# Hybrid decoder block on one core: expert rows stored at once by GpSimd's queue, and gathered back with an add inside the DMA

## The chip, the cores and the metric

The kernel runs on one core of one Trainium2 chip. The metric is the device time of one execution in microseconds (us), as the median of several runs; lower is better. The profile shows one execution on that core: TensorE (PE, with its weight loads PEld), VectorE (DVE), ScalarE (ACT), GpSimd (POOL) and SyncE (SP), and the DMA queues. SP's DMAs run in queue q1, GpSimd's in queue q0.

## The reference, cut to what matters

A decoder block for 512 tokens of width 1024. A token mixer and a LayerNorm come first; the change lies in the mixture of experts (16 experts in 4 groups, two experts for each token) and the last LayerNorm.

```python
# t: (512, 1024) after the first LayerNorm; combine: the two gates of each token, 0 elsewhere
h = jax.nn.silu(einsum("td,edf->tef", t, expert_w_gate)) * einsum("td,edf->tef", t, expert_w_up)
h = h * combine[:, :, None]
y = einsum("tef,efd->td", h, expert_w_down)          # expert_w_*: 1024 x 256, 256 x 1024
out = layer_norm(ALPHA * t + y, ln2_g, ln2_b)
```

Only the two chosen experts of a token count, so the kernel computes each expert on the at most 128 rows that chose it (an overflow branch, not taken here, does the rest).

## The kernel before

**Stages.** Up to about 650 us the kernel does the mixer, the first LayerNorm and the router. HT (four tiles of 128 tokens x 1024, float32) holds the normalized rows, with the last residual in it; hD is its copy in HBM. Then comes a loop over the experts, `for e in range(NE)`, and after it the last LayerNorm, tile by tile.

**The expert loop.** All float32 matmuls are done as three passes on split operands (high part, low part). Iteration e does, in an order written out by hand (`K` keeps it): `gate_up(e + 1, 0)`, the transposes of expert e's activations (L1303) and their split by ACT (L1304) and DVE (L1305, the low part FHL), `turn(e + 2, 0)`, `gate_up(e + 1, 1)`, `turn(e + 2, 1)`, `swiglu(e + 1)`, and `down(e, 0)`, `down(e, 1)`, whose passes need FHL. Between them stand three `splits()`, each of which splits one 1 MiB piece of weights (ACT L805 makes the high part, DVE L809 the low part, two of each).

**Weights.** Three pieces of 1 MiB for each expert, 48 in all, go through a ring of 16 raw buffers (`GR_RAW`); SP issues the DMAs (`eload`). When PE has used piece n, `release()` frees its buffer and issues the next load. From e = 3 on, five of the releases are withheld (`owed`): the ring shrinks to 11 buffers, and the 10 slots of 4 KB each are `kept`, nine for the expert outputs yo[3] to yo[11] and one for OHR.

**Token rows.** `gather(e)` is an indirect DMA of GpSimd that brings expert e's 128 rows from hD into one of five slots, XG[e % 5]. The `turn`s of an expert read its slot.

**Outputs of experts 0 to 11.** ACT scales the output into yo[e] (L1237). Experts 0 to 2 write into the gather slot XG[(e + 2) % 5] and SP stores it to yD in HBM at once; experts 3 to 11 stay in SBUF, and nine stores follow SP's last weight load (L1171). At the end of iteration 13 GpSimd issues eight indirect gathers of yD rows (L1347), two for each tile of 128 tokens, into buffers YG. Five of the eight gathered tiles are added to HT by GpSimd (L1352), three by DVE (two at L1309, one at L1399).

**Outputs of experts 12 to 15** never leave SBUF. They are put back to their tokens by matmuls with one-hot matrices, OHT[m], in `rows_of_last` (L1254). DVE makes OHT[m] at L1334 at the end of iterations 10 to 13, from OHR, a broadcast of the ranks out of HBM (rkD) that SP loads in one DMA at e = 3.

**The end.** For each tile i: `total(i)` adds the PSUM sums to HT (DVE L1364 twice, L1365) and ACT takes the squares; `inv_std(i)` (DVE L1372 to L1376); `half2(i)` finishes columns up to W2[i] on DVE (L1384) and the rest on ACT (L1383) and GpSimd (L1385, L1386), and SP stores both; `half1(i + 1)` (DVE L1379) starts the next tile. W2 is 512, 576, 704, 832. The order on DVE is total 0, (L1399), half1 0, then for each i: total i+1, inv_std i, half2 i, half1 i+1.

Of the kernel before, what the change touches and what calls it, by code (L numbers as in the profile page):

```python
# [13 lines left out]
BF16 = mybir.dt.bfloat16  # L14
I32 = mybir.dt.int32
AF = mybir.ActivationFunctionType
ALU = mybir.AluOpType
AX = mybir.AxisListType

D = 1024  # L20
S = 512
NT = 4
H = 8
KT = 8
NE = 16
# [5 lines left out]
CAP = 128  # L31
# [5 lines left out]
def body(ctx: ExitStack, tc: tile.TileContext, P: dict, out):  # L37
    nc = tc.nc
    V, A, G, T, SP = nc.vector, nc.scalar, nc.gpsimd, nc.tensor, nc.sync
# [24 lines left out]
    def reg(kb, *shape, dt=F32):  # L64

        n = int(np.prod(shape))
        o = int(round(kb * 256))
        assert o + n <= n_all, (kb, shape)
        return shaped(place(o, n, dt), shape)
# [22 lines left out]
    def carve(off, shape, dt, parts=128):  # L92
        half = dt in (F16, BF16)
        n = int(np.prod(shape))
        w = (n + 1) // 2 if half else n
        assert off + w <= n_all, (off, shape)
        return shaped(place(off, n, dt, parts), shape), off + -(-w // 8) * 8
# [42 lines left out]
    K = tc.keep_in_program_order  # L140
# [161 lines left out]
    p = pb()  # L302
# [5 lines left out]
    p = pb()  # L308
# [10 lines left out]
    early = [coff[0]]  # L319
# [21 lines left out]
    p = pb()  # L341
# [16 lines left out]
    p = pb()  # L358
# [47 lines left out]
    for h in range(H):  # L406
        if h % 2 == 0:
            w = wload(wcol("k", h // 2)) if h else w_k0
        p = chan_tile(w, h % 2)
        silu = conv_silu(p, 8 + h, KTr[:, h])  # L410
        p = pkk[h] = pb()
# [42 lines left out]
    for t in range(31):  # L454

        n, m = 31 - t, t + 1
# [21 lines left out]
    for cch in range(4):  # L478
# [3 lines left out]
        for j in range(2):  # L482
            h = cch * 2 + j
            p = chan_tile(w, j)
            conv_silu(p, h, QTr[:, h])
            p = pb()
# [4 lines left out]
            p = pb()  # L491
# [43 lines left out]
    for cch in range(4):  # L535
# [3 lines left out]
        for j in range(2):  # L539
            h = cch * 2 + j  # L540
            p = chan_tile(w, j)
            vT = scratch(S)
            conv_silu(p, 16 + h, vT)
            p = pb()
# [20 lines left out]
    for c in range(NT):  # L565
        cs = slice(c * 128, (c + 1) * 128)
        if c < NT - 1:
            for hh in range(2):
                hs = slice(hh * 4, hh * 4 + 4)
                p = pb()  # L570
# [3 lines left out]
        for hh in range(2):  # L574
            hs = slice(hh * 4, hh * 4 + 4)
            if c > 0:
                p = pb()
                for u in range(4):
                    T.matmul(p[:, u * 128:(u + 1) * 128], KTr[:, hh * 4 + u, cs], SS[:, hh * 4 + u], start=True, stop=True)
                for u in range(4):  # L580
                    h = hh * 4 + u
                    V.scalar_tensor_tensor(VT[:, c, h], p[:, u * 128:(u + 1) * 128], nG[:, h, c:c + 1], VT[:, c, h],
                                           op0=ALU.mult, op1=ALU.add)
                p = pb()
# [5 lines left out]
            p = pb()  # L590
# [3 lines left out]
            if c < NT - 1:  # L594
                p = pb()
# [4 lines left out]
                else:  # L600
                    for u in range(4):
                        h = hh * 4 + u
                        V.scalar_tensor_tensor(SS[:, h], SS[:, h], GL[:, h, c:c + 1], p[:, u * 128:(u + 1) * 128],
                                               op0=ALU.mult, op1=ALU.add)
            p = pb()
# [9 lines left out]
    for cch in range(4):  # L615
        w = wload(wcol("u", cch))
        for j in range(2):
            p = chan_tile(w, j)
# [18 lines left out]
    for c in range(NT):  # L637
# [4 lines left out]
        for h in range(H):  # L642
            V.scalar_tensor_tensor(QK[:, c, h], QK[:, c, h], ory[:, c, h:h + 1], Z[:, c, h * 128:(h + 1) * 128],
                                   op0=ALU.mult, op1=ALU.mult)
        for hh in range(2):
            hs = slice(hh * 4, hh * 4 + 4)
            p = pb()
# [16 lines left out]
    for hh in range(2):  # L664
        p = pb()
# [4 lines left out]
    for hh in range(2):  # L670
        p = pb()
        T.matmul(p, ones, WST[:, hh * 4:hh * 4 + 4], start=True, stop=True)
        for u in range(4):
            gi = hh * 4 + u
            V.scalar_tensor_tensor(EG[:, gi], p[:, u * 128:(u + 1) * 128], colT[:, 104 + gi:105 + gi], EG[:, gi],
                                   op0=ALU.mult, op1=ALU.add)
# [40 lines left out]
    for gi in range(8):  # L717
        p = pb()
        with tc.issue_after(done[23].ins):
            for i in range(NT):  # L720
# [4 lines left out]
                               op0=ALU.mult, op1=ALU.add)  # L725
# [9 lines left out]
    HT = reg(120, NT, D)  # L735
    for i in range(NT):
        SP.dma_start(HT[:, i, :], x_in[:, i, :])
    for cch in range(4):
        cols = slice(cch * 256, (cch + 1) * 256)
        if cch:  # L740
            w1 = wload(wcol("gdn", cch))
            for j in range(2):
                p = chan_tile(w1, j)
                A.activation(SIG[j], p, AF.Sigmoid)
        w2 = wload(P["w_dn_out"][0][:, cols])
        for j in range(2):
            p = chan_tile(w2, j, lambda k: OHI[:, :, k], lambda k: OLO[:, :, k])
            V.tensor_tensor(YT[j], p, SIG[j], ALU.mult)
        w3 = wload(wcol("gsgu", cch))
        for j in range(2):  # L750
            p = chan_tile(w3, j)
            A.activation(SIG[j], p, AF.Sigmoid)
        w4 = wload(P["w_sgu_out"][0][:, cols])
        for j in range(2):
            n = cch * 2 + j
            p = chan_tile(w4, j, lambda k: GHI[:, k], lambda k: UG[k][1])
# [17 lines left out]
    free, at, nload, last_load = deque(GR_RAW), {}, [0], [None]  # L774

    def eload():

        n = nload[0]
        if n >= len(order):
            return  # L780
        nload[0] += 1
        e, part = order[n]
        kb = at[n] = free.popleft()
        if part < 2:
            raw, lo = both(kb, 4, 512)
            ks = slice(part * 512, part * 512 + 512)
            SP.dma_start(raw[:, :, 0:FF], P["expert_w_gate"][0][e][ks].rearrange("(k p) f -> p k f", p=128))
            SP.dma_start(raw[:, :, FF:512], P["expert_w_up"][0][e][ks].rearrange("(k p) f -> p k f", p=128))
        else:
            raw, lo = both(kb, 2, D)  # L790
            last_load[0] = SP.dma_start(raw, P["expert_w_down"][0][e].rearrange("(k p) d -> p k d", p=128))
        raws[order[n]] = raw, lo
# [44 lines left out]
    p = pb()  # L837
# [40 lines left out]
    iof, irb, pid = late(16), late(128, dt=BF16), late(1)  # L878
# [135 lines left out]
    NL = 12  # L1014
    sli, idx, gsl = cst(NT, 2, dt=I32), cst(16, dt=I32), cst(16)
# [13 lines left out]
    p = pb()  # L1029
# [8 lines left out]
    XG = [reg(o, D) for o in (184, 188, 192, 0, 4)]  # L1038

    def gather(e):  # L1040
        if e < NE:
            return G.indirect_dma_start(out=XG[e % 5], out_offset=None, in_=hD,  # L1042
                                        in_offset=bass.IndirectOffsetOnAxis(ap=idx[:, e:e + 1], axis=0))
# [32 lines left out]
    with tc.If(most > CAP):  # L1076
# [12 lines left out]
        with tc.For_i(0, NE, 1) as eo:  # L1089
            wex = lambda nm, r: P[nm][0][bass.ds(eo, 1)].rearrange("o (k p) f -> p (o k) f", p=128)[:, r]  # L1090
            for b in range(1, NBLK):
                SP.dma_start(oi, iD[bass.ds(eo * (NBLK - 1) + (b - 1), 1)].rearrange("b p o -> p (b o)"))
                G.indirect_dma_start(out=OX, out_offset=None, in_=hD,
                                     in_offset=bass.IndirectOffsetOnAxis(ap=oi[:, 0:1], axis=0))
                for hh in range(2):
                    p = pb()
# [4 lines left out]
                p = pa()  # L1101
# [9 lines left out]
                p = pb()  # L1111
# [5 lines left out]
                for n in range(2):  # L1117
                    p = pa()
# [46 lines left out]
    FHL = carve(mixer_only, (2, 128), F32R)[0]  # L1165
    yD = dram.tile([ZROW + 1, D], F32, name="yD")
    Y_LAST, yo = [], {}
    E0 = 3

    def store(e):  # L1170
        SP.dma_start(yD[e * CAP:(e + 1) * CAP], yo[e])  # L1171

    OHT = [regr(o, S) for o in (188, 190, 192, 194)]
    def turn(e, hh):
# [9 lines left out]
        K(V.tensor_tensor(XGL[:, hs], v3(p), f_(XGH[:, hs]), ALU.subtract))  # L1184

    pgu = {}
    used, owed, kept = [0], [0], deque()

    def release():

        n = used[0]
        used[0] += 1
        if n == 0:
            return
        if owed[0]:
            owed[0] -= 1
            kept.extend((at[n], at[n] + 4))
        else:
            free.append(at[n])
            eload()  # L1200

    def kmm3(*args):
        K(T.matmul(args[0], args[1], args[3], start=args[5], stop=False))  # L1203
# [14 lines left out]
    def down(e, n):  # L1218
        wh, wl = ready[(e, 2)]
        p = pa()  # L1220
        ns = slice(n * 512, (n + 1) * 512)
        for f in range(2):
            kmm3(p, FHH[:, f], FHL[:, f], wh[:, f, ns], wl[:, f, ns], f == 0, f == 1)
        if n == 1:
            release()
        w_ = gsl[:, e:e + 1]
        if e >= NL:
            if n == 0:
                kb = free.popleft()
                Y_LAST.append((regr(kb, D), regr(kb + 4, D)))  # L1230
            yh, yl = Y_LAST[e - NL]
            K(A.activation(yh[:, ns], p, AF.Copy, scale=w_))
            K(V.scalar_tensor_tensor(yl[:, ns], p, w_, f_(yh[:, ns]), op0=ALU.mult, op1=ALU.subtract))
            return
        if n == 0:
            yo[e] = reg(kept.popleft(), D) if e >= E0 else XG[(e + 2) % 5]
        K(A.activation(yo[e][:, ns], p, AF.Copy, scale=w_))  # L1237
        if n == 1 and e < E0:
            store(e)

    def swiglu(e):
# [48 lines left out]
    A.activation(rkT, p[:(NE - NL) * NT, :128], AF.Copy)  # L1290
    SP.dma_start(rkD, rkT)
    for e in range(NE):
        if E0 <= e < NL and (e == E0 or not (e - E0) % 2 == 0):
            owed[0] += 1
        gate_up(e + 1, 0)
        if e == NE - 2:
            LNR2 = reg(free.pop(), 2, D)
            ln_rows("ln2_g", "ln2_b", LNR2)
        if e < NE - 2:
            splits()  # L1300
        p = pb()
        for f in range(2):
            K(T.transpose(p[:, f * 128:(f + 1) * 128], SGB[:, f * 128:(f + 1) * 128], ident))  # L1303
        K(A.activation(FHH, v3(p[:, 0:256]), AF.Copy))  # L1304
        K(V.tensor_tensor(FHL, v3(p[:, 0:256]), f_(FHH), ALU.subtract))  # L1305
        turn(e + 2, 0)
        if e == NE - 1:
            for n in range(2):
                K(V.tensor_tensor(HT[:, 0], HT[:, 0], YG[0][n], ALU.add))  # L1309
            rows_of_last(1, 0, (0, 1))  # L1310
        gate_up(e + 1, 1)
        splits()
        turn(e + 2, 1)
        if e <= E0:
            gather(e + 5)
        if e == E0:
            gather(e + 6)
        if e >= E0:
            gather(e + 7)
        if e == E0:  # L1320
            kept_rk = kept.popleft()
            OHR = reg(kept_rk, NE - NL, NT, 128, dt=BF16)
            SP.dma_start(OHR, bass.AP(tensor=rkD.tensor, offset=rkD.offset,
                                      ap=[[0, 128], [NT * 128, NE - NL], [128, NT], [1, 128]]))
        swiglu(e + 1)
        splits()
        down(e, 0)
        down(e, 1)
        if e == NE - 2:
            rows_of_last(0, 0, (0, 1))  # L1330
            rows_of_last(0, 1, (0, 1))
        if NL - 2 <= e < NE - 2:
            m = e - NL + 2
            K(V.tensor_scalar(OHT[m], OHR[:, m].rearrange("p i t -> p (i t)"), pid, None, op0=ALU.is_equal))  # L1334
        if e == NL:
            with tc.issue_after(last_load[0].ins):
                for m in range(E0, NL):
                    store(m)
        if e == NE - 3:
            YG = [yo[m] for m in range(E0, NL)] + [reg(kept_rk, D)]  # L1340
            while len(YG) < 8:
                kb = free.popleft()
                YG += [reg(kb, D), reg(kb + 4, D)]
            YG = [YG[i * 2:i * 2 + 2] for i in range(NT)]
            for i in range(NT):
                for n in range(2):
                    K(G.indirect_dma_start(out=YG[i][n], out_offset=None, in_=yD,  # L1347
                                           in_offset=bass.IndirectOffsetOnAxis(ap=sli[:, i, n:n + 1], axis=0)))
            for i in range(1, NT):
                for n in range(2):  # L1350
                    if i + n > 1:
                        K(G.tensor_tensor(HT[:, i], HT[:, i], YG[i][n], ALU.add))  # L1352


    out_v = out.rearrange("b (i p) d -> p (b i) d", p=128)
# [40 lines left out]
        rows_of_last(i, n, ALL, pool)  # L1396
    W2 = [512, 576, 704, 832]
    total(0)
    K(V.tensor_tensor(HT[:, 1], HT[:, 1], YG[1][0], ALU.add))  # L1399
    half1(0, W2[0])  # L1400
    for i in range(NT):
        if i + 1 < NT:
# [27 lines left out]
```

## Time and profile before

| | |
|---|---|
| time, median of 3 runs (lowest, highest) | 830.06 us (829.65, 832.38) |
| time of the profiled execution | 829.64 us |
| its span, first to last instruction | 827.9 us |
| busy of the span: PE, DVE, ACT, POOL | 94%, 65%, 46%, 13% |
| moved by DMA | 133.65 MB, mean 161 GB/s |
| of that by q1 (SP) and q0 (GpSimd) | 120.33 MB and 12.58 MB |
| mean granted clock of TensorE | 0.976 of full speed |

The profiled execution's time is 1.74 us more than its span; a change of the span is taken as a change of the time. Shares over the whole span are means over stages with different limits, so the expert loop (about 650 to 800 us) and the end (800 to 827.9 us) have to be read each for itself.

### The profile page before, as it was taken

How to read it: one execution, taken by the hardware profiler on the slowest of the kernel's cores; microseconds unless marked ns; L12 is line 12 of the kernel's file. 1: busy time of each engine (PE TensorE's matmuls, PEld its weight loads, DVE VectorE, ACT ScalarE, POOL GpSimd, SP SyncE). 2: the span in 40 equal slices, each digit the busy share in tenths (PEclk: the TensorE clock that was granted, in tenths of full speed). 3: DMA queues.
4: the chain of work that ended last, by engine and by line, in shares of the span. 5: the costliest groups of instructions: out<-in, count | busy, mean ns of one | idle time of the engine just before them, and what ended most of it. 6: DMA issues, size and time to landing. Idle time of an engine off the chain costs nothing.

```text
span 827.9 us, 10853 instructions
## 1 busy us (share of the span) xinstructions
PE 779.1 (94%) x4043; PEld 647.5 (78%) x4043; DVE 535.5 (65%) x1026; ACT 385.0 (46%) x612; POOL 106.7 (13%) x90
## 2 busy tenths in 40 slices
PE   8879999999999999999999999999994999999991
PEld 7567888787889988888788888888773788888780
DVE  3337882997575992547633332323578899999987
ACT  2485353453335542423322222222323899899843
POOL 0002002001100000000500000001031202110177
PEclk9998999999999999999999999999996999999996
DMA  9526336336260135343244333369818899999762
GB/s 225 87 59 169 79 81 143 84 69 154 46 139 2 51 72 95 94 102 77 99 129 103 103 101 103 102 241 331 291 52 260 297 382 388 367 341 307 280 250 101
DMA packets 110752, 133.65 MB, mean 161 GB/s; under 512 B 19780, under 2 KB 93032, under 8 KB 110696
## 3 DMA queue, kind: packets, MB, share of 16 engines
q1 hardware_dynamic: 107240, 120.33, 50.2%
q0 software_dynamic: 3456, 12.58, 4.3%
q8 instruction: 33, 0.54, 0.3%
q14 instruction: 23, 0.19, 0.1%
HBM read 120.82 MB, written 12.08 MB: 161 GB/s over the span
## 4 chain that ended last, share of the span: by engine, by line
PE 76%; issue 9%; DVE 9%; DMA 2%; ACT 2%; POOL 1%; POOLq 0%; DVEq 0%; SPq 0%; ACTq 0%
PE pa L237 16%; PE pa L236 16%; PE pa L235 16%; PE pa L1205 5%; PE pa L1203 4%; PE pa L1204 4%; PE pb L1181 2%; PE pb L525 1%; DVE r L809 1%; DVE r L386 1%; PE pb L607 1%; PE pb L592 1%; PE pb L509 1%; DMA r<-hD,r 1%; PE pb L414 1%
## 5 line engine op out<-in xcount | busy, mean ns | idle before, releaser
L235 PE MATMUL pa<-r,r 128*128 128x512 f32 (+1 forms) x712 | 280.1, 393 | 7.5 <-ACT r L149 7.3
L236 PE MATMUL pa<-r,r 128*128 128x512 f32 (+1 forms) x712 | 278.3, 391 | 2.2 <-DVE r L150 2.2
L237 PE MATMUL pa<-r,r 128*128 128x512 f32 (+1 forms) x712 | 277.5, 390 | 0.0
L150 DVE TENSOR_TENSOR r<-r,r 128x2048 fp32r<-128x2048 f32 (+2 forms) x48 | 102.8, 2148 | 134.6 <-ACT r L149 134.6
L235 PEld LDWEIGHTS pa<-r,r 128*128 128x128 f32 x712 | 134.4, 189 | 35.6 <-ACT r L149 8.1
L236 PEld LDWEIGHTS pa<-r,r 128*128 128x128 f32 x712 | 134.5, 189 | 29.5 <-DVE r L150 3.2
L237 PEld LDWEIGHTS pa<-r,r 128*128 128x128 f32 x712 | 134.3, 189 | 27.3 <-DVE r L232 0.4
L149 ACT ACTIVATE r<-r 128x2048 fp32r<-128x2048 f32 (+2 forms) x48 | 84.8, 1777 | 143.3 <-PE pa L236 82.0
L809 DVE TENSOR_TENSOR r<-r,r 128x1024 fp32r<-128x1024 f32 x96 | 117.1, 1222 | 5.6 <-ACT r L805 3.9
L805 ACT ACTIVATE r<-r 128x1024 fp32r<-128x1024 f32 x96 | 96.3, 1059 | 0.0
L1203 PE MATMUL pa<-r,r 128*128 128x512 f32 x192 | 78.2, 407 | 0.0
L1205 PE MATMUL pa<-r,r 128*128 128x512 f32 x192 | 75.9, 395 | 1.0 <-DVE r L1305 1.0
L1204 PE MATMUL pa<-r,r 128*128 128x512 f32 x192 | 75.6, 394 | 0.0
L386 DVE SCALAR_TENSOR_TENSOR r<-pa,r,r 128x511 f32<-128x511 f32 (+2 forms) x72 | 53.5, 743 | 15.7 <-ACT r L384 15.2
L1205 PEld LDWEIGHTS pa<-r,r 128*128 128x128 f32 x192 | 36.0, 188 | 9.9 <-DVE r L1305 1.9
L1203 PEld LDWEIGHTS pa<-r,r 128*128 128x128 f32 x192 | 36.3, 189 | 7.1 <-ACT r L1183 0.2
L1204 PEld LDWEIGHTS pa<-r,r 128*128 128x128 f32 x192 | 36.3, 189 | 6.9
L387 ACT ACTIVATE r<-r 128x512 f32<-128x512 f32 x24 | 15.1, 630 | 46.7 <-DVE r L386 42.9
L1042 POOL DMA_INDIRECT r<-hD,r x16 | 21.1, 1317 | 91.4 <-PE pb L1181 37.3
L758 POOL TENSOR_TENSOR r<-r,r 128x512 f32<-128x512 f32 x8 | 10.3, 1290 | 146.2 <-DVE r L757 142.0
L384 ACT ACTIVATE r<-pa,r 128x512 f32<-128x512 f32 x24 | 16.3, 680 | 25.2 <-PE pa L237 25.2
L1181 PE MATMUL pb<-r,r 128*128 128x128 f32 x128 | 20.2, 284 | 8.3 <-DMA r<-hD,r 8.2
(325 smaller groups left out, 899.0 us busy)
## 6 DMA issues: line engine op xcount, KB each, us to landing
r<-in_w_in_dram SPq DMA_DIRECT2D x29, 1024.0 KB, 8.9
r<-in_expert_w_gate_dram SPq DMA_DIRECT2D x32, 512.0 KB, 6.8
r<-in_expert_w_down_dram SPq DMA_DIRECT2D x16, 1024.0 KB, 8.4
r<-in_expert_w_up_dram SPq DMA_DIRECT2D x32, 512.0 KB, 8.4
yD<-r SPq DMA_DIRECT2D x12, 512.0 KB, 9.7
r<-in_x_dram SPq DMA_DIRECT2D x8, 512.0 KB, 5.9
r<-in_w_dn_out_dram SPq DMA_DIRECT2D x4, 1024.0 KB, 5.5
r<-in_w_sgu_out_dram SPq DMA_DIRECT2D x4, 1024.0 KB, 6.0
```

Source lines behind the costliest of these rows:

```text
L149: pin(A.activation(hi, raw, AF.Copy))
L150: pin(eng.tensor_tensor(lo, raw, f_(hi), ALU.subtract))
L235: pin(T.matmul(o, lh, rh, start=first, stop=False))
L236: pin(T.matmul(o, lh, rl, start=False, stop=False))
L237: pin(T.matmul(o, ll, rh, start=False, stop=last))
L386: V.scalar_tensor_tensor(acc[:, s:], p[:, :S - s], wc(3 - s), acc[:, s:], op0=ALU.mult, op1=ALU.add)
L805: K(A.activation(hi[:, s], raw[:, s], AF.Copy))
L809: K(V.tensor_tensor(lo[:, s], raw[:, s], f_(hi[:, s]), ALU.subtract))
L1181: K(T.transpose(p[:, u * 128:(u + 1) * 128], XG[e % 5][:, k * 128:(k + 1) * 128], ident))
L1203: K(T.matmul(args[0], args[1], args[3], start=args[5], stop=False))
L1204: K(T.matmul(args[0], args[1], args[4], start=False, stop=False))
L1205: K(T.matmul(args[0], args[2], args[3], start=False, stop=args[6]))
```

## The change

Every expert from 0 to 11 now writes its output into the gather slot XG[(e + 2) % 5], and GpSimd's queue, no longer SP's, stores it at once. No weight buffer is withheld, so the ring keeps 16 buffers. `gather(e + 5)` is issued in iteration e throughout. Behind expert 11's store GpSimd issues the eight gathers from yD, now with an add in the DMA, straight onto HT: first one for each of the four tiles, then the second ones. All additions of gathered rows by DVE and GpSimd go. OHR becomes four DMAs of 128 KiB, issued by SP in iteration 11; three of the four lie in slot XG[2] (192 to 195 KB), which holds yo[10] until it is stored. The OHT[m] are made one iteration later, at the end of iterations 11 to 14.

```diff
--- before.py
+++ after.py
@@ -1165,10 +1165,9 @@
     FHL = carve(mixer_only, (2, 128), F32R)[0]
     yD = dram.tile([ZROW + 1, D], F32, name="yD")
     Y_LAST, yo = [], {}
-    E0 = 3
 
     def store(e):
-        SP.dma_start(yD[e * CAP:(e + 1) * CAP], yo[e])
+        K(G.dma_start(yD[e * CAP:(e + 1) * CAP], yo[e]))
 
     OHT = [regr(o, S) for o in (188, 190, 192, 194)]
     def turn(e, hh):
@@ -1184,7 +1183,7 @@
         K(V.tensor_tensor(XGL[:, hs], v3(p), f_(XGH[:, hs]), ALU.subtract))
 
     pgu = {}
-    used, owed, kept = [0], [0], deque()
+    used = [0]
 
     def release():
 
@@ -1192,12 +1191,8 @@
         used[0] += 1
         if n == 0:
             return
-        if owed[0]:
-            owed[0] -= 1
-            kept.extend((at[n], at[n] + 4))
-        else:
-            free.append(at[n])
-            eload()
+        free.append(at[n])
+        eload()
 
     def kmm3(*args):
         K(T.matmul(args[0], args[1], args[3], start=args[5], stop=False))
@@ -1233,9 +1228,9 @@
             K(V.scalar_tensor_tensor(yl[:, ns], p, w_, f_(yh[:, ns]), op0=ALU.mult, op1=ALU.subtract))
             return
         if n == 0:
-            yo[e] = reg(kept.popleft(), D) if e >= E0 else XG[(e + 2) % 5]
+            yo[e] = XG[(e + 2) % 5]
         K(A.activation(yo[e][:, ns], p, AF.Copy, scale=w_))
-        if n == 1 and e < E0:
+        if n == 1:
             store(e)
 
     def swiglu(e):
@@ -1290,8 +1285,6 @@
     A.activation(rkT, p[:(NE - NL) * NT, :128], AF.Copy)
     SP.dma_start(rkD, rkT)
     for e in range(NE):
-        if E0 <= e < NL and (e == E0 or not (e - E0) % 2 == 0):
-            owed[0] += 1
         gate_up(e + 1, 0)
         if e == NE - 2:
             LNR2 = reg(free.pop(), 2, D)
@@ -1305,23 +1298,18 @@
         K(V.tensor_tensor(FHL, v3(p[:, 0:256]), f_(FHH), ALU.subtract))
         turn(e + 2, 0)
         if e == NE - 1:
-            for n in range(2):
-                K(V.tensor_tensor(HT[:, 0], HT[:, 0], YG[0][n], ALU.add))
             rows_of_last(1, 0, (0, 1))
         gate_up(e + 1, 1)
         splits()
         turn(e + 2, 1)
-        if e <= E0:
-            gather(e + 5)
-        if e == E0:
-            gather(e + 6)
-        if e >= E0:
-            gather(e + 7)
-        if e == E0:
-            kept_rk = kept.popleft()
-            OHR = reg(kept_rk, NE - NL, NT, 128, dt=BF16)
-            SP.dma_start(OHR, bass.AP(tensor=rkD.tensor, offset=rkD.offset,
-                                      ap=[[0, 128], [NT * 128, NE - NL], [128, NT], [1, 128]]))
+        gather(e + 5)
+        if e == NL - 1:
+
+            OHR = [reg(192 + m, NT, 128, dt=BF16) for m in range(NE - NL - 1)]
+            OHR.append(carve(early[0], (NT, 128), BF16)[0])
+            for m in range(NE - NL):
+                SP.dma_start(OHR[m], bass.AP(tensor=rkD.tensor, offset=rkD.offset + m * NT * 128,
+                                             ap=[[0, 128], [128, NT], [1, 128]]))
         swiglu(e + 1)
         splits()
         down(e, 0)
@@ -1329,27 +1317,16 @@
         if e == NE - 2:
             rows_of_last(0, 0, (0, 1))
             rows_of_last(0, 1, (0, 1))
-        if NL - 2 <= e < NE - 2:
-            m = e - NL + 2
-            K(V.tensor_scalar(OHT[m], OHR[:, m].rearrange("p i t -> p (i t)"), pid, None, op0=ALU.is_equal))
-        if e == NL:
-            with tc.issue_after(last_load[0].ins):
-                for m in range(E0, NL):
-                    store(m)
-        if e == NE - 3:
-            YG = [yo[m] for m in range(E0, NL)] + [reg(kept_rk, D)]
-            while len(YG) < 8:
-                kb = free.popleft()
-                YG += [reg(kb, D), reg(kb + 4, D)]
-            YG = [YG[i * 2:i * 2 + 2] for i in range(NT)]
-            for i in range(NT):
-                for n in range(2):
-                    K(G.indirect_dma_start(out=YG[i][n], out_offset=None, in_=yD,
-                                           in_offset=bass.IndirectOffsetOnAxis(ap=sli[:, i, n:n + 1], axis=0)))
-            for i in range(1, NT):
-                for n in range(2):
-                    if i + n > 1:
-                        K(G.tensor_tensor(HT[:, i], HT[:, i], YG[i][n], ALU.add))
+        if NL - 1 <= e < NE - 1:
+            m = e - NL + 1
+            K(V.tensor_scalar(OHT[m], OHR[m].rearrange("p i t -> p (i t)"), pid, None, op0=ALU.is_equal))
+        if e == NL - 1:
+
+            for n in range(2):
+                for i in range(NT):
+                    K(G.indirect_dma_start(out=HT[:, i], out_offset=None, in_=yD,
+                                           in_offset=bass.IndirectOffsetOnAxis(ap=sli[:, i, n:n + 1], axis=0),
+                                           compute_op=ALU.add))
 
 
     out_v = out.rearrange("b (i p) d -> p (b i) d", p=128)
@@ -1396,7 +1373,6 @@
         rows_of_last(i, n, ALL, pool)
     W2 = [512, 576, 704, 832]
     total(0)
-    K(V.tensor_tensor(HT[:, 1], HT[:, 1], YG[1][0], ALU.add))
     half1(0, W2[0])
     for i in range(NT):
         if i + 1 < NT:
```

## Rows read from the trace of the kernel before

**Rows 1.** Windows, three expert cycles: length, busy by engine, clock, DMA share, GB/s.

```profile
664.00:673.40 9.40, 9.40 (x49) 7.78 (x48) 9.30 (x11) 8.56 (x12) 0.94 (x1) 1.00 1.07 380
739.10:748.50 9.40, 9.40 (x48) 7.79 (x47) 9.03 (x10) 8.66 (x13) 0.00 (x0) 1.00 1.05 366
776.60:786.70 10.10, 9.73 (x49) 7.77 (x48) 10.00 (x14) 7.10 (x11) 2.61 (x2) 1.00 0.53 193
```

**Rows 2.** Waits of PE, 640 to 828 us: total, times, longest (us).

```profile
PE pa L1205 <- DVE r L1305: 1.0, 2, 0.6
```

**Rows 3.** Chain that ended last, from 796 us: start, us, what.

```profile
800.01 1.32 DVE r L1364 x4
...
801.50 3.03 DVE r L1399
...
804.59 2.67 issue
807.25 1.31 DVE r L1364 x4
...
810.35 2.82 DVE r L1379
813.17 1.23 DVE r L1364 x4
...
817.24 1.23 DVE r L1364 x4
```

**Rows 4.** Timeline of GpSimd: start, us, operation, [idle before it, and what ended it].

```profile
670.40 0.94 POOL L1042 DMA_INDIRECT r<-hD,r  x1 [18.79 <-DMA yD<-r]
...
733.70 1.57 POOL L1042 DMA_INDIRECT r<-hD,r  x1 [7.81 <-PE pb L1181]
...
788.58 0.94 POOL L1347 DMA_INDIRECT r<-yD,r  x1 [0.30 <-issue]
...
798.68 13.86 POOL L1352 TENSOR_TENSOR r<-r,r 128x1024 f32<-128x1024 f32 x5 [3.50 <-DMA r<-yD,r]
...
817.03 1.20 POOL L1385 TENSOR_TENSOR r<-r,r 128x448 f32<-128x448 f32 x1 [1.40 <-ACT r L1383]
```

**Rows 5.** Timeline of DVE: start, us, operation.

```profile
767.18 0.48 DVE L1334 TENSOR_SCALAR r<-r,r 128x512 fp32r<-128x512 bf16 x1
...
769.97 0.42 DVE L1305 TENSOR_TENSOR r<-pb,r 128x256 fp32r<-128x256 f32 x1
...
780.73 0.42 DVE L1305 TENSOR_TENSOR r<-pb,r 128x256 fp32r<-128x256 f32 x1
...
795.20 2.47 DVE L1309 TENSOR_TENSOR r<-r,r 128x1024 f32<-128x1024 f32 x2
...
816.30 0.94 DVE L1379 SCALAR_TENSOR_TENSOR r<-r,r,r 128x704 f32<-128x704 f32 x1
```

**Rows 6.** Timeline of PE: start, us, operation.

```profile
766.97 0.38 PE L1303 MATMUL pb<-r,r 128*128 128x128 f32 x2
...
771.29 0.39 PE L1205 MATMUL pa<-r,r 128*128 128x512 f32 x1
...
807.97 1.98 PE L1254 MATMUL pb<-r,r 128*128 128x512 f32 x8
```

**Rows 7.** Timeline of ACT: expert 10's two scalings.

```profile
754.89 1.27 ACT L1237 ACTIVATE r<-pa,r 128x512 f32<-128x512 f32 x2
```

**Rows 8.** Line L1042, GpSimd's gathers from hD: issue to landing.

```profile
DMA to landing us min/median/max: 4.0/7.7/10.0
```

**Rows 9.** Line L1171, SP's stores to yD: issue to landing.

```profile
DMA to landing us min/median/max: 8.1/9.7/10.6
```

**Rows 10.** Line L1347, GpSimd's gathers from yD: issue to landing.

```profile
DMA to landing us min/median/max: 4.7/9.6/10.1
```

**Rows 11.** Windows of 6 us, columns as in rows 1.

```profile
714.00:720.00 6.00, 6.00 (x29) 4.90 (x28) 5.93 (x7) 5.32 (x8) 1.57 (x1) 1.00 1.10 352
...
774.00:780.00 6.00, 6.00 (x33) 4.96 (x32) 5.93 (x8) 5.67 (x8) 0.00 (x0) 1.00 1.02 418
```

## The prediction

> **What bounds the kernel now.** I read the windows by expert cycle first. In the loop one expert takes 9.4 us, PE is busy all of it at full clock, and DVE 9.0 to 9.3 us of it; the DMA engines are as full, at a share of 1.05 to 1.07 and 366 to 380 GB/s [rows 1]. PE, which can't be shortened by this change, sets the pace; DVE and DMA stand close behind. The waits of PE then show that the loop loses almost nothing: 1.0 us in two waits, both for DVE's FHL [rows 2], one of them in the cycle of expert 13, where PE is busy 9.73 of 10.1 us [rows 1].
>
> Third, the end. PE's last matmul ends at 809.95 [rows 6], but the span ends at 827.9 (its table row): 18 us without PE. The chain there runs over DVE, and the four totals start 7.2, 5.9 and 4.1 us apart [rows 3]. The timelines say why the first two rounds are long. GpSimd is adding gathered rows from 798.68 to 812.54, five additions of 2.8 us [rows 4]. DVE's own addition, L1399, takes 3.03 us in that time [rows 3], while two of the same shape took 2.47 us together before GpSimd began [rows 5]. L1379 takes 2.67 and 2.82 us [rows 3]; with 704 columns and no additions beside it, it takes 0.94 [rows 5]. So a DVE operation with two SBUF inputs is held up until GpSimd's addition is done.
>
> The Trainium skill says as much (SBUF — State Buffer, Who interferes with whom): such an instruction and a GpSimd instruction that reads SBUF exclude each other for a whole instruction. The trace agrees, with 3.03 us against 1.2.
>
> **The end, part by part.** Removed: GpSimd's 13.86 us of additions [rows 4] and L1399. The third round (4.07 us, from 813.17 to 817.24) has a total, an inv_std, a half2 and a half1 and nothing held up long [rows 3]; I take it for rounds two and three. The first round has no inv_std and no half2: 1.49 us for the total (800.01 to 801.50) and about 0.7 us for a half1 of 512 columns (0.94 us for 704 [rows 5], by columns), 2.2 us. The last total then starts at 800.01 + 2.2 + 4.07 + 4.07 = 810.35 instead of 817.24 [rows 3]. PE hardly stops that: its last sums are there at 809.95 [rows 6], and only the total's second half needs them. That is a gain of 6.9 us. GpSimd's half2 operations (1.20 us for 448 columns [rows 4]) now stand closer to DVE's SBUF operations; a collision costs between nothing and one such operation, two or so can happen ahead of the last total, so 0 to 2.4 us; I take 0.8. From the last total to the end the work is what it was.
>
> L1309's 2.47 us lie in iteration 15, where DVE has idle time; I count nothing for it. If that cover were not there it would be 2.5 us more gain.
>
> **The stores and the loop.** Stores on GpSimd cost POOL 0.94 to 1.57 us each, by its gathers [rows 4]; POOL is idle 7.8 us before each gather, so this is hidden. The wait of a store for ACT L1237 holds back the next gather only, which has three cycles until its turn. A gather into a slot waits for that slot's store (as the one at 670.40 did [rows 4]), 8 to 10.6 us [rows 9], while 28 us stand between them. SP gets rid of nine stores and waits for nothing new until iteration 11.
>
> Where the trace is against the change is the DMA's load. Each cycle now moves three pieces, a gather and a store, 4.19 MB in 9.4 us or 446 GB/s, through iteration 10, because no load is withheld and no store put off. The row nearest to this mix is the cycle at 664 us, which had all of it, and moved 380 GB/s [rows 1]. Bounds: 352 and 418 GB/s [rows 11]. At 380, each of ten cycles leaves 0.62 MB over, 6.2 MB; less 1.0 MB, since the first two cycles have no gather (the one at 670.40 is the first [rows 4]): 5.2 MB. With a full ring the last load leaves after gate_up(11, 0), two cycles ahead of the L1303 at 766.97 [rows 6], so at 748.2. Gathers and stores (112 GB/s) leave 268 GB/s to drain the rest: 19.4 us, until 767.6. Weights don't mind: a piece is split twelve pieces, 37.6 us, after its issue.
>
> **The moved load of OHR does.** Its DMAs wait for store 10. ACT has scaled expert 10 at 756.16 [rows 7]; the store lands some 8 us later [rows 8, 9], at 764. Then they stand behind the rest of the weights in SP's queue: at 380 GB/s, about 768.5. DVE reaches the first L1334, in iteration 11, at 767.18 less the 0.4 us of the one that iteration 10 no longer has [rows 5], 766.8. So DVE stands 1.7 us. Behind it in DVE's order are the splits and FHL of expert 12 (769.97 to 770.39 [rows 5]), which PE needs at 771.29 [rows 6]: 0.9 us spare, 1.2 with most of those 0.4. PE loses 0.5 us there; and the next FHL comes 10.76 us later [rows 5] against a cycle of 9.4, so it loses 1.36 more. Before it lost about 0.5 in that place [rows 1, 2]. Net loss 1.4 us. Bounds: at 418 GB/s the rest is gone by 757 and the stall is nothing (net gain 0.3); at 366 the same sum (6.5 MB at 254 GB/s) gives 774, a stall near 8 us and a net loss near 7.5.
>
> **The accumulating gathers.** Store 11 is ready at 765.5 (one cycle after expert 10's), lands by 775 [rows 9]; four gathers leave 1.24 us apart [rows 4], the second of tile 0 when its first has landed. No row has an add in the DMA. Below it is a plain gather, 4.7 to 10.1 us [rows 10]; above, twice that, since the destination is moved both ways. With 9.6 us the sums of tile 0 are there at 794, with twice 4.7 too; total 0 needs them at 800. I take nothing for it; with twice 9.6 us it would be 813, 13 us late.
>
> **The sum.** Span 827.9 − 6.9 + 0.8 + 1.4 = 823.2; with the 1.74 us around it 824.9 us, against 829.64 for the profiled execution, which lies 0.4 below the median of 830.06.
>
> **The rivals.**
> - *OHR is much later* (the rate is near 372): with a stall of 5 us PE loses 5.2 − 0.5 = 4.7 us, which gives 828.2, no change that can be told. For it: most saturated windows lie below 380. Against it: the mix with stores had 380 and 418.
> - *Slower: the adds in the DMA are slow.* From a landing of 16 us on, tile 0's sums come at 775 + 32 = 807, and the 6.9 us are used up; at twice the loaded median of 9.6 us it is 824.9 + 13 = 838, less the 1.4 us that the delay hides, 836. For it: no row shows such a DMA. Against it: the DMA queues are nearly empty then, and the gathers of before landed as early as 4.7 us [rows 10].
> - *Weights come late.* At 352 GB/s the rest is 7.8 MB at 748, drained at 240 GB/s: 32 us, with the ordinary landing of 8 about 40 us against 37.6. A few us of wait on top of a long OHR stall: 833 to 836.
> - *The contention stays:* if GpSimd's half2 operations hold DVE as the additions did, only L1399 itself (1.2 us) and part of L1379 go; about 828.
>
> A rule of the Trainium skill speaks against stores on GpSimd's queue (SBUF — State Buffer, the "DVE blocks DMA" trap): its descriptors are written by GpSimd's cores and starve while DVE holds the shared port. Here the trace shows gathers of 1.57 us beside DVE's splits and 0.94 otherwise [rows 4]; by that the store of expert 10 would be 0.6 us later, which is within the bounds of OHR's landing.
>
> **How the numbers follow.** What a measurement of this kernel can tell is 0.3%, 2.5 us. The forecast (stall of 0 to 4 us, 821.5 to 827) has 0.62; late OHR 0.15; slow adds 0.10; late weights 0.07; contention that stays 0.06. The forecast is nearly all faster, a part of late OHR too: faster 0.67, same 0.18 (late OHR, contention), slower 0.15. The range 821 to 831 leaves out most of the two slow cases and a little below.
>
> **What would show it.** Right: no POOL additions between 798 and 812, totals 2 to 4 us apart, the last starting near 811 to 812; DVE idle before the first L1334, ended by the load of rkD. Wrong: PE waiting for ACT L805 or DVE L809 behind a weights DMA in the loop; total 0 waiting for the yD gathers; the last total still near 817; or L1334 without a wait, and then 823.

## The result, and the profile after

The changed kernel takes 835.66 us (median of 16 runs, 831.51 to 841.08), the kernel before 829.85 (16 runs, 825.86 to 832.72). The ratio is 1.0075, 95% interval 1.0052 to 1.0097: slower by a little, but clear of the noise, where the prediction said 824.9 us and faster, and outside its range.

The profiled execution has a span of 833.9 us, 6.0 more than before. Three stretches make it up. The first gather from hD starts at 635.60 instead of 633.82; no edit touches what lies before it, and this stretch differs by up to 8 us between the profiles of this study (that gather starts at 631.3 to 639.3), so experiments are compared from that gather on, and by ratios of medians. From there to the first total the change costs 9.9 us (176.1 against 166.2). From the first total to the end it saves 5.7 (22.2 against 27.9).

The waits of DVE and PE, 650 to 840 us (total, times, longest), show one wait that was not there before: PE's longest was 0.6 us [rows 2], DVE's longest 1.0. Two answers, DVE's first:

```profile
DVE r L1322 <- DMA r<-rkD: 10.3, 1, 10.3
...
PE pa L1200 <- DVE r L1298: 9.9, 2, 9.3
```

L1322 makes OHT[0] (L1334 before); L1298 makes FHL (L1305 before). The chain says what released it (start, us, what):

```profile
762.51 0.56 POOL yD L1170
763.07 12.18 DMA yD<-r
775.53 2.94 DMA r<-rkD
...
779.00 1.23 DVE r L809
...
781.39 0.43 DVE r L1298
781.87 0.79 PE pa L1200
782.66 0.43 PE pa L1198
```

A store of yD, then OHR (r<-rkD), then one split and FHL, then PE. The store is that of expert 10, and SP waits for nothing but it before OHR: its last weight load is out at 760.9. ACT's timeline and SP's waits:

```profile
756.00 1.26 ACT L1232 ACTIVATE r<-pa,r 128x512 f32<-128x512 f32 x2
```

```profile
SPq L1311 <- DMA yD<-r: 14.3, 1, 14.3
```

ACT has scaled expert 10 at 757.26. Its store leaves 5.8 us later, at 763.07, lands 12.2 us after that, and OHR lands 2.9 us after its own issue. (SP issues one of OHR's four DMAs early, at 662.68; the other three stand behind store 10.) The windows show what else it costs (columns as in [rows 1]):

```profile
758.00:767.00 9.00, 9.00 (x46) 7.45 (x45) 8.67 (x10) 8.27 (x13) 2.77 (x4) 1.00 1.07 381
767.00:776.00 9.00, 5.55 (x30) 4.32 (x28) 1.30 (x2) 7.12 (x10) 0.48 (x1) 0.97 0.81 330
776.00:786.00 10.00, 4.13 (x11) 3.28 (x12) 7.33 (x10) 0.69 (x1) 7.92 (x4) 0.52 0.80 147
```

DVE is busy 1.30 of 9 us. After PE's pause of 9.3 us the granted clock is at its lower level of 1.2 GHz (0.52 over that window), and some nine matmuls come 0.43 us apart instead of 0.23 (the chain above): 1.8 us more. In the last window, that of the adding gathers, the DMA engines move 147 GB/s at a share of 0.80; with plain DMAs alone they moved 381 at 1.07.

GpSimd's timeline tells why the store was late. In [rows 4] a gather waited for a store once; here the two alternate:

```profile
663.23 0.58 POOL L1170 DMA_DIRECT2D yD<-r  x1 [10.51 <-ACT r L1232]
672.13 0.98 POOL L1042 DMA_INDIRECT r<-hD,r  x1 [8.32 <-PE pa L1200]
673.11 0.58 POOL L1170 DMA_DIRECT2D yD<-r  x1
683.32 1.49 POOL L1042 DMA_INDIRECT r<-hD,r  x1 [9.63 <-DMA yD<-r]
684.81 0.58 POOL L1170 DMA_DIRECT2D yD<-r  x1
...
751.85 0.59 POOL L1170 DMA_DIRECT2D yD<-r  x1
760.95 1.57 POOL L1042 DMA_INDIRECT r<-hD,r  x1 [8.51 <-issue]
762.51 1.16 POOL L1170 DMA_DIRECT2D yD<-r  x2
```

The gathers are not among the operations whose order is kept. They stand on GpSimd's queue as early as they can: gather e + 6 right behind store e - 1 and ahead of store e. It fills the slot that store e - 1 empties, so it waits until that store has landed (8.1 to 10.0 us, median 8.9), and store e waits behind it. (The profile names the store as the releaser in two of the nine waits and something else in the others, but each gather starts 8.9 to 10.3 us behind the issue of the store ahead of it.) Stores leave every 11.1 us (663.23 to 751.85 in eight steps), while an expert takes 9.4 in experiment 1, and store 10 leaves at about 763 instead of 757.

The end went as forecast (chain; [rows 3] before):

```profile
811.72 1.32 DVE r L1341 x4
...
813.99 1.31 DVE r L1341 x4
...
817.81 1.23 DVE r L1341 x4
...
822.22 1.23 DVE r L1341 x4
```

Totals 2.3, 3.8 and 4.4 us apart, 10.5 together; before 17.2.

### The profile page after: what moved, and what is told of

Read it like the earlier page. It is cut to its first block, busy times and chain, and to the rows that moved or that the text cites. A ratio compares the mean times of both kernels' runs of the same rounds, so it can differ in the third digit from the quotient of the medians.

```text
span 833.9 us, 10867 instructions
## 1 busy us (share of the span) xinstructions
PE 779.1 (93%) x4043; PEld 646.6 (78%) x4043; DVE 527.4 (63%) x1023; ACT 385.0 (46%) x612; POOL 106.1 (13%) x97
## 5 line engine op out<-in xcount | busy, mean ns | idle before, releaser
L1042 POOL DMA_INDIRECT r<-hD,r x16 | 19.9, 1242 | 102.2 <-PE pa L1200 35.3
L758 POOL TENSOR_TENSOR r<-r,r 128x512 f32<-128x512 f32 x8 | 12.5, 1558 | 142.7 <-DVE r L757 136.0
```

## The experiments

Each experiment is timed beside the kernel before on the same chip. The median of that kernel is 829.3 us in experiments 1 to 4, 827.7 in 5 to 8 and 829.5 in 9 to 11. All compute the whole of the reference.

**1. The loop's gathers in program order.**

```diff
-        gather(e + 5)
+        if e + 5 < NE:
+            K(gather(e + 5))
```

> Edit: the loop's gathers are kept in program order, so gather e+6 no longer stands ahead of store e+1 on GpSimd's queue; nothing else. Theory A (the order on GpSimd's queue: in the changed kernel each store waits, through the gather ahead of it, until the store before it has landed, so the stores fall behind by 1.5 us per expert): store 10 leaves GpSimd within 2 us of ACT's scaling of expert 10, lands 8 to 10 us later, OHR about 3 us after that, DVE's wait for rkD falls from 10.3 to 2 to 5 us, PE's wait from 9.3 to 1 to 4 us; 827 to 829 us against 835.7 of the changed kernel. Theory B (DMA bandwidth alone makes store 10 late): the stores leave on time but store 10 still lands 15 us or more after the scaling, PE loses 7 us or more; 833 us or more.

Measured 836.69 us, ratio 1.0091 (1.0062 to 1.0121). DVE's wait for rkD is 9.9 us, PE's longest 9.0. GpSimd's and SP's timelines:

```profile
751.35 0.57 POOL L1170 DMA_DIRECT2D yD<-r  x1 [7.19 <-ACT r L1232]
752.22 1.35 POOL L1042 DMA_INDIRECT r<-hD,r  x1 [0.30 <-issue]
760.75 0.57 POOL L1170 DMA_DIRECT2D yD<-r  x1 [7.18 <-ACT r L1232]
```

```profile
763.68 2.88 SPq L788 DMA_DIRECT2D r<-in_expert_w_up_dram  x1
766.73 3.00 SPq L791 DMA_DIRECT2D r<-in_expert_w_down_dram  x2
770.09 1.30 SPq L1312 DMA_DIRECT2D r<-rkD  x3
```

The stores now leave on time, every 9.4 us, and land in 6.3 to 8.1 us. But SP is still issuing weights until 769.7, and OHR lands 11.0 us after its issue. So theory A is right about the stores and wrong that they alone made OHR late. Theory B's size of PE's wait is right, and its reason (store 10 landing 15 us late) is wrong: what is late is SP's queue. With the stores on time the weights finish later: their last issue ends 130.4 us after the first gather of hD, against 125.3 in the changed kernel. That the earlier stores take that much of the DMA engines is the likely reason, and is not shown by itself.

**2. OHR loaded in iteration 3**, into one weight buffer withheld for it.

```diff
-        if e == NL - 1:
+        if e == 3:
-            OHR = [reg(192 + m, NT, 128, dt=BF16) for m in range(NE - NL - 1)]
-            OHR.append(carve(early[0], (NT, 128), BF16)[0])
+            OHR = [reg(kept[0] + m, NT, 128, dt=BF16) for m in range(NE - NL)]
# in release()
+        if n == 11:
+            kept.append(at[n])
+            return
```

> Edit: OHR is loaded in iteration 3 into one weight buffer withheld for it (the ring has one buffer less), not behind store 10; nothing else. Theory A and theory B both say that the wait for OHR is all that the loop lost: no DVE wait for rkD, PE waits under 1 us after 660 us, TensorE's clock stays at full in the loop, time 835.7 less 9.3 less 1.8 (nine matmuls at half clock behind the stall) or 824 to 826 us. Theory C (weights late as well: the DMA engines at 380 GB/s can't keep up and the OHR stall only hid it): ACT or DVE waits for a weights DMA in iterations 11 to 14, PE loses 3 us or more, 828 us or more.

Measured 829.25 us, ratio 1.0011 (0.9986 to 1.0036). No wait for rkD, but another at the same instruction:

```profile
DVE r L1323 <- DMA yD<-r: 4.3, 1, 4.3
```

OHT[0] and OHT[1] lie in the slot of yo[9], and store 9, which is late too, has not landed. PE loses 3.4 us at most at a time, 4.0 in all. So theories A and B missed a second wait that stood in the shadow of the first; no weights were late (theory C).

**3. The kernel before with only the adding gathers.**

```diff
-                    K(G.indirect_dma_start(out=YG[i][n], ...))
+                    K(G.indirect_dma_start(out=HT[:, i], ..., compute_op=ALU.add))
# n outside, i inside; the additions at L1309, L1352 and L1399 go
```

> Edit: the kernel before with only its gathers of yD replaced by the eight adding ones onto HT, and the additions of DVE and GpSimd gone; stores, ring and OHR as before. Theory A: the end gains what it gained in the changed kernel, 27.9 less 22.2 or 5.7 us from the first total to the last instruction: 824 us against 829.85. Theory D (the adds in the DMA are too slow for this place: they start only at 784 us and move 150 to 195 GB/s): total 0 or a later total waits for the gathers, the gain is 0 to 3 us, 827 to 830.

Measured 828.02 us, ratio 0.9982 (0.9961 to 1.0004). Theory D holds. DVE's timeline at total 0:

```profile
803.32 0.69 DVE L1354 SCALAR_TENSOR_TENSOR r<-pb,r 128x512 f32<-128x512 f32 x1 [5.12 <-DMA r<-yD,r]
```

The gathers start only at 782 us, behind the deferred stores, and total 0 waits 5.1 us for them. The adding gathers need the stores early.

**4. Both edits: gathers in program order and OHR in iteration 3.**

> Edit: both, the loop's gathers in program order and OHR loaded in iteration 3. Theory A: the order on GpSimd's queue cost only through OHR, so the same as with OHR early alone, 824 to 826 us. If the late stores also cost elsewhere (the adding gathers start behind store 11, and the last totals may wait for them), this one is 1 to 3 us faster than OHR early alone.

Measured 824.05 us, ratio 0.9936 (0.9918 to 0.9953). That is the time of theory A, but not its reason: it had this kernel and the one with OHR early alone at the same time, and this one is 5.2 us faster, because the order on GpSimd's queue also cost through store 9, for which DVE no longer waits. PE's waits after 650 us are those of [rows 2] again:

```profile
PE pa L1203 <- DVE r L1301: 1.0, 2, 0.6
```

From the first gather of hD to the first total it takes 165.8 us (before 166.2, changed 176.1). So the waits of DVE for OHR and for store 9 were all that the loop lost.

**5. OHR on GpSimd's queue** (gathers in program order, OHR still behind store 10).

```diff
-                SP.dma_start(OHR[m], bass.AP(...))
+                K(G.dma_start(OHR[m], bass.AP(...)))
```

> Edit: the loop's gathers in program order, as in the first experiment, and OHR's four loads on GpSimd's queue behind store 10, not on SP's; nothing else. Theory F (with the stores on time OHR came 11 us after its issue because it stood behind the rest of the weights in SP's queue): on GpSimd's queue it lands 3 to 5 us after store 10 has landed, DVE's wait for it falls from 9.9 to 0 to 4 us, PE loses 0 to 3 us, 825 to 829 us. Theory G (no queue matters, any DMA lands late while the DMA engines are full): the wait stays at 7 us or more, 832 us or more.

Measured 827.77 us, ratio 0.9987 (0.9959 to 1.0015). DVE's wait:

```profile
771.17 0.49 DVE L1323 TENSOR_SCALAR r<-r,r 128x512 fp32r<-128x512 bf16 x1 [2.36 <-DMA r<-rkD]
```

OHR lands 5.7 to 6.7 us after its issue, a little over theory F's 3 to 5, against 11.0 on SP's queue; PE waits 3.2 us in three times instead of 9.6. Theory F holds: in the first experiment it was SP's queue that OHR stood in. From the first gather of hD, OHR's first issue comes at 129.2 us here and at 130.8 there, so 5.5 of the 7.0 us by which DVE goes on earlier here lie behind the issue.

**6. The stores on SP's queue** (otherwise as experiment 4).

```diff
-        K(G.dma_start(yD[e * CAP:(e + 1) * CAP], yo[e]))
+        SP.dma_start(yD[e * CAP:(e + 1) * CAP], yo[e])
```

> Edit: gathers in program order and OHR early, as in the fourth experiment (824.05 us), and the stores on SP's queue, not on GpSimd's. If the queue matters: SP's queue runs some 10 us late behind the weights, so the stores leave and land later than 8 us after the scaling, DVE's first L1334 of before (OHT[0], in the slot of store 9) waits a few us, the adding gathers start 5 us or more later and total 0 may wait; 826 to 830 us. If it doesn't: 823 to 825 us.

Measured 825.65 us, ratio 0.9980 (0.9952 to 1.0008); by the ratio behind experiment 4, but from the first gather of hD to the end it takes 188.1 us and experiment 4 188.0. The stores land in 10.1 to 13.8 us, DVE waits 1.5 us for store 9, and the first adding gather is issued 1.9 us later than in experiment 4 (141.9 against 140.0 us after the first gather of hD). Which queue stores matters little; inconclusive by the medians.

**7. Additions by GpSimd and DVE** (otherwise as experiment 4: plain gathers, but early).

```diff
-                    K(G.indirect_dma_start(out=HT[:, i], ..., compute_op=ALU.add))
+                    K(G.indirect_dma_start(out=YG[i][n], ...))
+                    ...
+                        K(G.tensor_tensor(HT[:, i], HT[:, i], YG[i][n], ALU.add))
```

> Edit: gathers in program order and OHR early, as in the fourth experiment (824.05 us), and the eight gathers of yD plain, into freed weight buffers, with the additions by GpSimd (five) and DVE (three) as in the kernel before; the gathers still start behind store 11. Theory H (an addition on GpSimd holds up DVE's operations with two SBUF inputs wherever it runs): the five additions now run in iterations 13 to 15 beside the weight splits, L809 grows beside them to 2 us and more, PE loses 2 to 5 us there, and L1399 and the three DVE additions cost about 1 us at the end; 826 to 830 us. Rival: the additions are hidden once the gathers are early, and the add in the DMA brings nothing; 823 to 825 us.

Measured 830.56 us, ratio 1.0033 (1.0009 to 1.0056). Theory H. GpSimd's and DVE's timelines:

```profile
787.92 14.39 POOL L1340 TENSOR_TENSOR r<-r,r 128x1024 f32<-128x1024 f32 x5
```

```profile
785.88 2.48 DVE L809 TENSOR_TENSOR r<-r,r 128x1024 fp32r<-128x1024 f32 x2
...
791.18 6.39 DVE L809 TENSOR_TENSOR r<-r,r 128x1024 fp32r<-128x1024 f32 x2
```

Two splits that take 2.48 us by themselves take 6.39 beside the additions, and PE waits for it. So the add in the DMA itself is worth 5.3 us here (193.3 against 188.0 us from the first gather of hD to the end, in this experiment and in the fourth), not just its early place.

**8. OHT elsewhere** (experiment 2, with OHT in a freed weight buffer; the gathers ahead of the stores as in the changed kernel).

```diff
+        if e == NL - 1:
+            kb = free.popleft()
+            OHT = [regr(kb + 2 * m, S) for m in range(NE - NL)]
```

> Edit: OHR early, as in the second experiment (829.25 us, where DVE still waited 4.3 us for a store), and the one-hot matrices OHT in a freed weight buffer, not in the gather slots of experts 9 and 10; the gathers stay where the scheduler put them, ahead of the stores. If the late stores cost only through the slots that OHR and OHT share with them: no DVE wait at L1334 of before, PE waits about 1 us, 823 to 826 us. If they cost elsewhere too (weights, adding gathers): 827 us or more.

Measured 825.22 us, ratio 0.9964 (0.9942 to 0.9986); no DVE wait where OHT is made (L1326 in this kernel), PE waits 1.0 us, first gather to first total 165.1 us. The late stores cost only through the slots that OHR and OHT share with them.

**9. A version from the experiments**: adding gathers and full ring, stores on SP's queue, gathers in program order, OHR in iteration 3, OHT in a freed buffer.

> Edit: of the changed kernel the adding gathers and the full ring stay; the stores are on SP's queue, the gathers in program order, OHR is loaded in iteration 3 and OHT lies in a freed weight buffer. Theory A: PE's only waits in the loop are the 1.0 us of the kernel before, no DVE wait for rkD or yD, totals 1.7, 3.7 and 4.4 us apart, and with no direct store on GpSimd's queue the span ends 2.4 us after the last store's issue, not 3.5: 7.5 us less than before from the first gather of hD to the end, 821 to 823.5 us beside 829. If the SP stores hold up the weights or the adding gathers: 824 us or more.

Measured 823.70 us, ratio 0.9933 (0.9914 to 0.9953); 186.9 us from the first gather of hD to the end, 7.2 less than before. DVE waits for neither rkD nor yD and PE 1.0 us, as theory A had it; the first two totals are 2.3 us apart, not 1.7. Faster than both kernels, and not to be told from experiment 4.

**10. One small store on GpSimd's queue in the kernel before.**

```diff
-    zeros = K(SP.dma_start(yD[ZROW:ZROW + 1]...))
+    zeros = K(G.dma_start(yD[ZROW:ZROW + 1]...))
```

> Edit: the kernel before with its one 4 KB store of zeros to yD on GpSimd's queue instead of SP's; nothing else. If a direct store on GpSimd's queue, whatever its size, lengthens the end of the program: the span ends about 3.5 us after the last store's issue instead of 2.44, and the time is 1 us longer, which is hardly more than noise. If the 1 us of the changed kernel comes of something else: 2.4 us again.

Measured 830.38 us, ratio 1.0002 (0.9984 to 1.0020). The span ends 2.9 us after the start of the last store's issue, as with stores on SP (2.8 to 3.1), not 3.8. (The expectation counts from the end of that issue, 0.33 us later.) That a store on GpSimd's queue lengthens the end whatever its size is refuted.

**11. The changed kernel with its stores on SP's queue**, nothing else.

> Edit: the changed kernel with its stores on SP's queue, not on GpSimd's; nothing else, so OHR still waits for store 10 in the slot of that store. If the queue of the stores was the cause: DVE's wait for rkD falls to 4 us or less, 825 to 829 us. If the wait of OHR behind the store and the weights is the cause, whichever queue stores: DVE waits 7 us or more again, PE loses 6 us or more, 832 to 837 us.

Measured 833.28 us, ratio 1.0045 (1.0027 to 1.0063). DVE waits 9.8 us for rkD, PE 8.8. SP's last store is out at 770.2, OHR is issued at 778.14, when store 10 has landed, and L1322 starts at 781.23. So GpSimd's queue is not needed for the loss: on SP's queue the store is late behind the weights and takes 13.0 us to land, and OHR waits for it all the same.

## Why the prediction was wrong

- **The end** was right. Predicted from the first to the last total 10.3 us and 0.8 of collisions; measured 10.4 in experiments 4 and 9 and the changed kernel (10.5 by its chain). From the last total to the end it is 1.0 us longer than before (11.8 against 10.7), which was not foreseen. Net 5.7 instead of 6.1.
- **The adding gathers** were right: they land 8.0 to 9.5 us after their issue in the changed kernel and 6.7 to 13.2 in experiments 4 and 9, and no total waits for them in any of the three. The bound that the destination moves both ways is near the rate that the windows show: 147 to 195 GB/s where plain DMAs move 380.
- **The DMA's load** was right in rate from 673 on (379 to 391 GB/s in every window to 767) and right that weights are not late for PE. The two windows ahead of that, from 654, moved 363 and 340.
- **The moved load of OHR is the step that failed**: the mechanism was named, its size was not. Predicted: DVE stands 1.7 us, PE loses a net 1.4. Measured: 10.3, and 9.3 + 1.8 for the clock, a net 9.9 from the first gather of hD to the first total. Put into the sum for the 1.4, that makes the span 823.2 - 1.4 + 9.9 = 831.7 us; the 0.4 of the end and the 1.8 ahead of the first gather make up the rest to the 833.9 measured. The prediction's own bound, a stall near 8 us and a net loss near 7.5 at 366 GB/s, was passed although the rate was 380.
- In the changed kernel the way from the scaling of expert 10 to OHR's landing took 21.2 us, where the prediction had 12.3. The store left 5.8 us late where it had nothing; it landed in 12.2 us where it had 8, near the low end of [rows 9], whose median is 9.7; and OHR's own landing took 2.9 us where it had 0.9, besides a wait behind the weights that did not come. Why this store took 12.2 us is not shown; it left 0.6 us behind store 9.
- Two readings under it were wrong. **"The wait of a store for ACT L1237 holds back the next gather only"**, and that 28 us stand between a store and the gather into its slot, took the order of the source for the order on GpSimd's queue; a gather stood ahead of each store and tied it to the landing of the one before. That put store 10 at 763 instead of 757. And **the 5.2 MB left at 748** were counted from nothing at 654 and at 380 GB/s throughout. In the kernel before, the loads of 640 to 655 us landed 7.9 to 9.8 us after their issue, those of 740 to 760 in 4.3 to 7.3, which suggests that a rest was there already; and the windows of 363 and 340 leave about 0.5 MB more, an estimate from these rates. How the error divides is not shown. Experiment 1 shows its size: weights were being issued until 769.7, 764.2 in the clock of the kernel before (its first gather starts 5.5 us later), and OHR landed at 781, or 775.6, not at 768.5.
- Either error alone is enough: in the changed kernel OHR waits for store 10, with no weight ahead of it; with the stores on time, it stands behind the weights. That is why experiment 1 gained nothing.
- Smaller things: the first buffer of the ring becomes gather slots 3 and 4 after its first use, so the rings of 16 and 11 are 15 and 10. The load counted as the last leaves where the prediction has it. The 2.67 us read as L1379 is called issue in the chain; DVE's timeline has 2.88 and 2.90 for L1379, which says the same. At 418 GB/s the prediction's sum, with its 1.0 MB taken off, gives 754 and not 757; the stall is nothing either way. A store cost GpSimd 0.54 to 0.59 us to issue, not 0.94 to 1.57, and not every gather beside DVE's splits took 1.57: in the kernel before, those at 650.67 and 681.41 took 0.94 and 0.98.

## What to carry to other kernels

When a load is moved behind a store, look at what stands ahead of the store on its queue and ahead of the load on its own, in the order as compiled and not as written; two queues can each make it late by the same amount, and then mending one shows nothing. Small early data, such as OHR, belongs where no late buffer is reused. Additions that would run on GpSimd beside a full DVE are better done in the DMA, if the rows are there early enough for its half speed.

## What the runs showed of the hardware

- **Which queue a small DMA stands in counted for much here.** OHR took 11.0 us to land behind weights on SP's queue and 5.7 to 6.7 on GpSimd's, both at a DMA share of 1.07. The Trainium skill (DMA: Bandwidth & Descriptors, Issuing engines are not separate DMA queues) says that DMAs from several engines run on the same 16 engines, and that issuing from several saves only issue time. For bytes the runs agree (about 380 GB/s either way); for the latency of a small transfer in a backlog they don't, and the measurement decides.
- **SP's single issues grow long in the full stretch**: they took up to 4.7 us in the changed kernel and 5.4 in experiment 1, where loads issued from 740 to 762 landed 12.0 to 14.0 us later. In the kernel before, from 740 to 760, where loads landed in 4.3 to 7.3 us, they took 0.37 to 0.51. That the backlog holds SP up is the reading that fits; no wait names it. The longest in the changed kernel:

```profile
718.44 4.71 SPq L787 DMA_DIRECT2D r<-in_expert_w_gate_dram  x1
```

- **With the twelve stores on GpSimd's queue the span ends 3.8 to 4.1 us after the start of the last output store's issue**, with none there 2.8 to 3.1. One small store there doesn't do it (experiment 10). No wait in the profile names it; the cause stays open.
